# The first feed-forward layer's down products with tokens standing, and its partial sums turned back on chip

## The chip, the cores and the metric

The kernel runs on one core of one Trainium2 chip. The metric is device time in microseconds (us) of one execution. The kernel before ran three times: 843.07, 843.22 and 842.23 us, median 843.07. One further execution was recorded by the hardware profiler; its trace is the source of every other number.

In what follows PE is TensorE's matrix multiplication and PEld its weight loads, DVE is VectorE, ACT is ScalarE, POOL is GpSimd and SP is SyncE, which here only issues DMA transfers. A matmul multiplies a *standing* operand of 128 x 128, which is loaded first, with a *moving* one of up to 512 columns. The result is added up in PSUM, which has eight banks of 128 x 512 floats. SBUF is the on-chip memory that all engines read and write; HBM is the memory outside.

## The reference

One layer of a decoder trunk on 512 tokens of 1024 channels, in float32: a feed-forward layer, a token mixer, and another feed-forward layer, each between two RMS norms.

```python
def swiglu(x, w_gu, w_down):
    gate, up = jnp.split(x @ w_gu, 2, axis=-1)
    return (jax.nn.silu(gate) * up) @ w_down

# the layer, in short
x = x + 0.5 * rms_norm(swiglu(rms_norm(x, ffn1_pre_g), ffn1_w_gu, ffn1_w_down), ffn1_post_g)
h = rms_norm(x, mix_pre_g)
x = x + rms_norm(hybrid_mixer(h, ...), mix_post_g)
x = x + 0.5 * rms_norm(swiglu(rms_norm(x, ffn2_pre_g), ffn2_w_gu, ffn2_w_down), ffn2_post_g)
```

The hidden width is 2816, that is 22 chunks of 128. The mixer projects h to a recurrent branch (xl, its gates), to q and kv of a windowed attention, and to a gate gt. This case is about the down product of the first layer (`w_down`, 2816 x 1024) and about how its result reaches the residual sum.

## The kernel before

**Precision.** A product of two floats is three matmuls: each operand is split into a high part (an ACT copy into a format that PE multiplies at full rate) and a low part (a DVE subtraction), and high x high, high x low and low x high are added in PSUM.

**Layout.** Up to the end of the first layer, activations lie with channels in the 128 partitions and the 512 tokens along the row. One channel chunk of the residual stream `xT` is 128 x 512. A down product with *weights standing* gives that same layout; one with *tokens standing* gives 128 tokens by 512 channels.

**The hidden chunks come in groups** (`GROUPS1`: 0-3, 4-7, 8-11, 12-15, 16-21).

- Group 0 is computed plainly (`classic`). Its down product follows at once: for each of eight channel chunks c, four hidden chunks times three matmuls of 512 columns (lines 506 to 508), 96 in all. ACT copies each result to a stage tile and POOL sends it to HBM (line 1416), in `in_hbm`, one tile for two channel chunks. Between these products ACT and DVE make operands for the next groups (`n1.sums`, `n1.lows`), and after the fourth `xT` itself goes out to HBM (`lend`), so that its buffers can hold weights.
- Groups 1 to 4 (the first four chunks of the last) use a scheme with seven products where eight are usual, on both levels. `octo` computes gate and up with tokens standing (line 951), turns the result with DVE transposes (line 961) and stores it to HBM. While the octo of group g runs, the hidden chunks of group g-1 are read back and their sums and differences formed (`seven_forms_of`), and after it comes `seven_down` for group g-1. That is three times: for groups 1, 2 and 3.
- `seven_down` (line 1087) makes seven products into eight banks: A, B, Dd and E_, two banks each. With `by_channels` (line 1347) each product is 24 matmuls of 256 columns, weights standing. After the products named a12, s3, s2, s4, a22 and s1, ACT copies two banks to stages (line 1113) and POOL adds them to the HBM tiles (line 1116), accumulating in the transfer. The last of them goes to two places.
- After the last seven_down, a `quad` handles hidden chunks 20 and 21 (line 881, seven products of 24 matmuls), while chunks 16 to 19 come back from HBM and are split (lines 820 and 821).
- The last down product takes the six chunks 16 to 21, weights standing, channel chunk by channel chunk: c = 0 and 1 together, then 2, 3, 4. To each, `Residual.chunk` adds what the other groups had left in HBM: five reads at line 1380 and three at line 1389, of 256 KB each, issued by SP. Chunks 5 to 7 are left to `boundary`, which computes them in halves of 256 tokens: the sum of squares over all channels (line 709) closes, PE reduces it (line 550), and scaling, residual sum and the mixer's first four products (the xl weights) follow in an interleaved order.

**The order of work** is written out by hand: each engine executes in the order in which the program issues. Weights are an ordered list of *raws* (one load by SP at line 175 each, into one of five buffers) and *units* (a high part by ACT, a low part by DVE, some by POOL). `W.take` hands out the next unit and runs the splitting four units ahead. When the last unit of a raw has been split, the next raw is loaded, unless the list `W.owed` has an entry, which is then called in place of the load. Buffers are handed out in turn: a tile that asks for one waits until all readers of the tile that had it are done. `W.later` puts off a call by so many takes.

**Other work around the change.** `decay_factor` (lines 1274 to 1294, a dozen tiny DVE operations and two ACT functions) runs beside the octo of group 1. In the last down product, c = 0 loads the recurrent gates' weights (line 1309) and builds the attention masks (`masks`, lines 1324 to 1329, POOL and one DVE cast); at c = 3 the gates are split (`split_gates`, lines 1316 and 1317) and POOL reads `xT` back (`give_back`, line 1357, two transfers of 1 MB). The mixer starts with the kv product, then the convolution, whose result ACT and POOL split (line 1475) for the gate products (line 1456). The second layer's down products have tokens standing already (`by_tokens`, lines 1884 to 1886).

Of the kernel before, what the change touches and what calls it, by code (L numbers as in the profile page):

```python
# [122 lines left out]
def tile_layer(ctx: ExitStack, tc: tile.TileContext, out: bass.AP, **ins: bass.AP):  # L123
# [222 lines left out]
    for g, (f0, f1) in enumerate(GROUPS1):  # L346
        if g == 0:
            for f in range(2, f1, 2):
                add_gate_up(w1, f, "a")
        else:  # L350
            add_octo(w1, f0, "a")
            if g > 1:
                add_seven_down(ins["ffn1_w_down"], GROUPS1[g - 1][0], "a")
            if f1 < FC:
                continue
            add_quad(w1, f0 + 4, "a")
        for c in range(0, KD, 2):
            for add in add_cols(ins["ffn1_w_down"], c, f1 - f0, f"ad{g}", f0):
                add()
# [435 lines left out]
    def like(t, x):  # L795

        return t.rearrange("p (a b) -> p a b", a=2) if len(x.shape) == 3 else t

    class Hidden:


        def __init__(self, name, nxt):
            self.name, self.nxt, self.hs, self.g, self.u = name, nxt, {}, {}, {}

# [12 lines left out]
        def split(self, f):  # L817
            us, n = self.u.pop(f), f"{self.name}{f}"
            hh, hl = (spare.pop(), spare.pop()) if spare else (t2k(f"hh{n}", F32R), t2k(f"hl{n}", F32R))
            act.copy(hh, us)  # L820
            dve.tensor_sub(hl, us, hh.bitcast(F32))
            self.hs[f] = (hh, hl)

        def high(self, name, x):

            hh = t2k(f"hh{name}", F32R)
            act.copy(like(hh, x), x)
            self.forms[name] = hh, x

        def low(self, name):  # L830
# [3 lines left out]
            dve.tensor_sub(like(hl, x), x, like(hh.bitcast(F32), x))  # L834
# [171 lines left out]
        def seven_forms_of(self, f, h_hbm, at=(1, 2.5, 3.5, 4.5, 5.5, 6)):  # L1006
# [3 lines left out]
            def fetch():  # L1010
# [6 lines left out]
                z = wide(f"hx{self.name}{f}")  # L1017
                for s in range(2):
# [69 lines left out]
    def seven_down(hid, f, one, part, forms, ahead, beside={}, keep=False):  # L1088
# [7 lines left out]
        for n, (banks, form, blocks) in enumerate(((A, "a11", []), (Dd, "s3", [(1, 1)]), (B, "a12", [(0, 0)]), (A, "s2", [(1, 0)]),  # L1096
# [10 lines left out]
            for i in range(2 if form in (("s3", "s2") if keep else ("a12", "s3", "s2", "s4", "a22", "s1")) else 0):  # L1107
# [6 lines left out]
                for half, dh in blocks:  # L1114
                    o = part(half, dh, i)
                    pool.dma_start(o, st.rearrange("p (a b) -> p a b", a=2) if len(o.shape) == 3 else st, accum_op=ALU.add)  # L1116
# [217 lines left out]
    in_hbm = [hbm.tile([P, 2, 2, T // 2], F32, name=f"yp_a{i}") for i in range(KD // 2)]  # L1334

    def in_halves(t):
        return t.rearrange("p (a b) -> p a b", a=2)

    def by_channels(banks, w, h, first):

        (hi, lo), (hh, hl_) = w, h
        for m in range(4):
            o, ms = banks[m // 2][:, HALF[m % 2]], slice(m * P, (m + 1) * P)
            for k in range(2):
                js = HALF[k]
                for i, (a, x) in enumerate(((hi, hh), (hi, hl_), (lo, hh))):
                    pe.matmul(o, a[:, k, ms], x[:, js], start=first and i + k + m % 2 == 0, stop=k == 1 and i == 2, skip_group_check=True)  # L1347
# [14 lines left out]
    for g, (f0, f1) in enumerate(GROUPS1):  # L1362
        if g:
            h_hbm[f0] = hid.octo(f0, hid.seven_forms_of(before, h_hbm[before]) if g > 1 else {2: [lambda: decay.append(decay_factor())]})
            if g > 1:
                seven_down(hid, before, by_channels, lambda half, dh, i: in_hbm[2 * dh + i][:, half], hid.forms, AHEAD - 1)
            if f1 == FC:
                W.owed = [lambda: None] * 2
# [3 lines left out]
            xs = hid.last_chunks(f0, h_hbm[f0], {})  # L1372
            ka, nka = decay[0]
        else:
            xs = hid.classic(f1, banks, {})
        if f1 == FC:
            res = Residual("r1", lambda c: half_g[:, c:c + 1])
            for c in range(5):
                parts[c] = t2k(f"yp_a{c}")
                sync.dma_start(in_halves(parts[c]), in_hbm[c // 2][:, :, c % 2])  # L1380
        for c in range(KD):
            if f1 == FC and c == 0:
                load_gates()
            if f1 == FC and c == 0:
                neg = masks()
            if f1 == FC and c == 1:
                for i in range(5, KD):
                    parts[i] = t2k(f"yp_a{i}")
                    sync.dma_start(in_halves(parts[i]), in_hbm[i // 2][:, :, i % 2])
            if f1 == FC and c == 1:  # L1390
                preload(AF.Sqrt)
            if f1 == FC and c == 3:
                split_gates()
            if f1 == FC and c == 3:
                x_tiles[:] = give_back()
            if f1 == FC and c >= KD - LATE:
# [11 lines left out]
            if g == 0 and c in (0, 1, 3, 4):  # L1408
                (n1.sums if c in (0, 3) else n1.lows)(2 + c // 3)
            if g == 0 and c == 3:  # L1410
                lend(x_tiles)
                W.load(2)
            if g == 0:
                st = t2k("stage")
                act.activation(st, b, AF.Copy, scale=-1.0 if c >= KD // 2 else 1.0)
                pool.dma_start(in_hbm[c // 2][:, :, c % 2], in_halves(st))
            else:
                res.chunk(c, b, parts[c])
# [61 lines left out]
    mx.spread()  # L1480
    R = mx.R
# [563 lines left out]
```

## Time and profile before

| What | Value |
| --- | --- |
| Median of three runs | 843.07 us (842.23 to 843.22) |
| Profiled execution, own time | 842.55 us |
| Its span in the trace | 840.8 us |
| Mean granted clock of PE | 0.999 |
| PE busy | 832.2 us, 99% |
| DVE busy | 723.8 us, 86% |
| ACT busy | 520.9 us, 62% |
| POOL busy | 162.6 us, 19% |
| Layer 1's three downs on the chain start at | 155.01, 213.27 and 271.53 us |
| The quad, the last down product | 291.69 to 311.84 us, from 311.84 us on |

The page's span counts from the first to the last instruction; the device time is 1.75 us longer in this execution. An engine's share of busy time says how much room it has on average, not when. The *chain* is the sequence of work that ended last, followed back from the end of the program: an engine that stands in it with 96% could only have finished earlier by having less work, while an idle gap of another engine costs nothing. Rows of a timeline give start, duration, engine, line, operation and tiles; a bracket at the end is the idle time of that engine just before, with what ended it. Matmul rows overlap: their pace is the distance between starts.

### The profile page before, as it was taken

What the parts mean: (1) busy time and instruction counts of PE and PEld (TensorE: products, weight loads), DVE (VectorE), ACT (ScalarE), POOL (GpSimd) and SP (SyncE); (2) the same over time, 40 slices, a digit from 0 to 9 for tenths busy, and PEclk for the clock granted to TensorE, in tenths of its full rate; (3) what the DMA queues carried; (4) which work ended last, traced back from release to release, by engine and by line L of the source; (5) the groups of instructions that cost most, each with busy time, mean ns of one, the idle gap of its engine ahead of it and who ended that gap; (6) DMA issues with size and microseconds to landing.
All of it is one profiled execution on the core that took longest, in us unless ns stands there. A gap on an engine that the chain in (4) does not pass through costs nothing.

```text
span 840.8 us, 12378 instructions
## 1 busy us (share of the span) xinstructions
PE 832.2 (99%) x4504; PEld 718.9 (85%) x4504; DVE 723.8 (86%) x1026; ACT 520.9 (62%) x821; POOL 162.6 (19%) x178
## 2 busy tenths in 40 slices
PE   9999999999999999999999999999999999999996
PEld 8988888988988998987788899888888888888885
DVE  4978999998989965879889589799999899898996
ACT  6646756666666655556797456536758667666562
POOL 2023000140320333304531052002004114032001
PEclk9999999999999999999999999999999999999999
DMA  7249429398595799323511131169439939769842
GB/s 252 77 128 347 135 79 318 80 251 267 123 255 186 167 261 331 93 62 108 157 51 51 51 105 47 50 129 290 179 106 232 317 92 257 253 149 258 305 140 101
DMA packets 123614, 143.73 MB, mean 171 GB/s; under 512 B 23897, under 2 KB 81569, under 8 KB 123041
## 3 DMA queue, kind: packets, MB, share of 16 engines
q1 hardware_dynamic: 109232, 111.86, 42.0%
q0 software_dynamic: 14176, 30.94, 17.0%
q8 instruction: 35, 0.57, 0.3%
q14 instruction: 27, 0.21, 0.1%
q10 hardware_dynamic: 144, 0.13, 0.0%
HBM read 100.45 MB, written 40.89 MB: 168 GB/s over the span
## 4 chain that ended last, share of the span: by engine, by line
PE 96%; DVE 2%; DMA 1%; SPq 0%; issue 0%; ACT 0%; DVEq 0%; ACTq 0%
PE aa L951 10%; PE ab L951 10%; PE db L951 5%; PE da L951 5%; PE yaa L1347 3%; PE bb L951 3%; PE ba L951 3%; PE yda L1347 2%; PE ya L506 2%; PE ya L507 2%; PE ya L508 2%; PE aa L881 1%; PE a_first L1206 1%; PE yab L1884 1%; PE yab L1885 1%; PE yab L1886 1%
## 5 line engine op out<-in xcount | busy, mean ns | idle before, releaser
L1116 POOL DMA_DIRECT2D yp_a<-stage x42 | 36.8, 1064 | 182.6 <-ACT stage L1113 158.8
L1116 POOL DMA_DIRECT2D yp_b<-stage x42 | 36.4, 1084 | 144.3 <-ACT stage L1113 117.8
L506 PE MATMUL ya<-hha,whi_ad 128*128 128x512 f32 x62 | 24.1, 389 | 0.0
L507 PE MATMUL ya<-hla,whi_ad 128*128 128x512 f32 x62 | 24.1, 389 | 0.0
L508 PE MATMUL ya<-hha,wlo_ad 128*128 128x512 f32 x62 | 24.1, 389 | 0.0
L686 POOL TENSOR_TENSOR acca_r<-acca_r,sq_r 128x512 f32<-128x512 f32 x6 | 8.1, 1357 | 61.7 <-ACT sq_r L536 61.7
L1900 POOL DMA_DIRECT2D yp_b<-stage x8 | 4.3, 548 | 67.1 <-ACT stage L1899 67.1
L524 PE MATMUL an<-xh_mx,whi_xl 128*128 128x256 f32 x64 | 15.9, 289 | 0.0
L525 PE MATMUL an<-xh_mx,wlo_xl 128*128 128x256 f32 x64 | 15.5, 283 | 0.0
L2003 POOL TENSOR_TENSOR last<-yp,grow 128x512 f32<-128x512 f32 x3 | 3.9, 1290 | 57.2 <-DVE yp L1993 57.2
L2000 ACT ACTIVATE ysq<-yp 128x512 f32<-128x512 f32 (+1 forms) x8 | 4.8, 606 | 16.2 <-DVE yp L1993 16.2
L506 PE MATMUL gt<-xh_mx,whi_gt 128*128 128x512 f32 x32 | 14.3, 445 | 0.0
L508 PEld LDWEIGHTS ya<-hha,wlo_ad 128*128 128x128 f32 x62 | 11.6, 188 | 2.4
L506 PEld LDWEIGHTS ya<-hha,whi_ad 128*128 128x128 f32 x62 | 11.6, 188 | 2.4
L507 PEld LDWEIGHTS ya<-hla,whi_ad 128*128 128x128 f32 x62 | 11.6, 188 | 2.4
L536 ACT ACTIVATE sq_r<-yp_a 128x256 f32<-128x256 f32 (+1 forms) x10 | 5.0, 502 | 12.9 <-DVE yp_a L676 5.9
L506 PE MATMUL pq<-xh_mx,whi_q 128*128 128x512 f32 x32 | 12.8, 399 | 0.0
L506 PE MATMUL pub<-xh_f,whi_bu 128*128 128x512 f32 x32 | 12.6, 395 | 0.0
L508 PE MATMUL gt<-xh_mx,wlo_gt 128*128 128x512 f32 x32 | 12.6, 394 | 0.0
L506 PE MATMUL pgb<-xh_f,whi_bg 128*128 128x512 f32 x32 | 12.6, 393 | 0.0
L507 PE MATMUL gt<-xl_mx,whi_gt 128*128 128x512 f32 x32 | 12.6, 392 | 0.0
L508 PE MATMUL pgb<-xh_f,wlo_bg 128*128 128x512 f32 x32 | 12.5, 390 | 0.0
(2014 smaller groups left out, 3468.8 us busy)
## 6 DMA issues: line engine op xcount, KB each, us to landing
yp_a<-stage POOLq DMA_DIRECT2D x50, 256.0 KB, 9.1
yp_b<-stage POOLq DMA_DIRECT2D x50, 256.0 KB, 9.0
h_a<-za SPq DMA_DIRECT2D x16, 256.0 KB
hxa<-h_a SPq DMA_DIRECT2D x16, 256.0 KB
h_b<-zb SPq DMA_DIRECT2D x16, 256.0 KB
hxb<-h_b SPq DMA_DIRECT2D x16, 256.0 KB
xn<-in_x SPq DMA_DIRECT2D x8, 256.0 KB
xT_hbm<-xT POOLq DMA_DIRECT2D x2, 1024.0 KB, 9.8
```

The source lines that it names most:

```text
L506: pe.matmul(ps, hi[:, k, :], xh, start=start, stop=False)
L507: pe.matmul(ps, hi[:, k, :], xl, start=False, stop=False)
L508: pe.matmul(ps, lo[:, k, :], xh, start=False, stop=stop)
L524: pe.matmul(ps[:, sl], hi[:, k, :], xh, start=k == 0 and not goes_on, stop=False, skip_group_check=True)
L525: pe.matmul(ps[:, sl], lo[:, k, :], xh, start=False, stop=False, skip_group_check=True)
L881: pe.matmul(o, w[:, k, js], x, start=first and i + j + k == 0, stop=k == 3 and i == 2, skip_group_check=True)
L951: pe.matmul(b[tb], x[:, blk], w[:, k, :], start=first and q + k + j == 0, stop=q + k == 2 and j == 2, skip_group_check=True)
L1116: pool.dma_start(o, st.rearrange("p (a b) -> p a b", a=2) if len(o.shape) == 3 else st, accum_op=ALU.add)
L1206: pe.matmul(banks[j][:, HALF[0]], ws[j][part][:, k, :], n1.xs[k][xpart][:, HALF[0]], start=k == 0 and part == xpart, stop=stop and k == KD ...
L1347: pe.matmul(o, a[:, k, ms], x[:, js], start=first and i + k + m % 2 == 0, stop=k == 1 and i == 2, skip_group_check=True)
L1884: pe.matmul(banks[i], hh[:, js], hi[:, k, :], start=first and k == 0, stop=False, skip_group_check=True)
L1885: pe.matmul(banks[i], hh[:, js], lo[:, k, :], start=False, stop=False, skip_group_check=True)
```

## The change

All of layer 1's down products but the last one change to tokens standing, so that their results lie with tokens in the partitions, in eight HBM tiles `rows_hbm[tb, dh]` (token block tb of 128, half dh of the channels).

- **Group 0:** `first_down` takes 128-token blocks of the hidden chunks as standing operand and the weights, 512 channels, as moving one: two halves x four hidden chunks x four token blocks x three, again 96 matmuls of 512 columns. Its weights come in four units of two raws. The hidden chunks are split in the dealt order of tokens that the octo's results have (`in_blocks`). The work that stood between the products (`sums`, `lows`, `lend`) stands after (half, chunk) 0,1 to 1,0.
- **seven_down:** `by_dealt_tokens` makes each product of 12 matmuls of 512 columns. The hidden chunks are read back in two transfers instead of four, and read in dealt order with access patterns of four dimensions (`by_blocks`).
- **The last seven_down** is called with `hold`: products a22 and s1 are neither copied nor accumulated; their four banks stay in PSUM (`held`), which leaves out four copies and six accumulating transfers of 256 KB.
- **The eight reads of partial sums** (lines 1380 and 1389) are gone. For the first half of the channels, `read_rows(0)` reads four tiles of 256 KB at step 0 of the quad, into the tile named R and the three accumulators; `turn_sums(0)` at step 4 adds two held banks and transposes all four in blocks of 32 x 32, and `move_sums(0)` puts the blocks in place with 16 transfers of 64 KB from SBUF to SBUF, every second one by POOL, the others by SP. For the second half, `read_rows(1)` reads into a buffer of raws, `turn_sums(1)` (four adds, four transposes) stands ahead of the last down product, its target is another buffer of raws, and `move_sums(1)` stands at c = 1. `W.owed` has two loads, then `read_rows(1)`, then nothing, where it had two entries that do nothing.
- **Moved:** `decay_factor` from the octo of group 1 to that of group 2; `masks` and `split_gates` from c = 0 and c = 3 into the mixer, ahead of the convolution.

The core of the diff:

```diff
+            for dh in range(2):
+                r = W.raw(lambda dh=dh: load_raw([ins["ffn1_w_down"][0, :f1 * P, HALF_D[dh]]], f1, T, f"ad0{dh}"))
+                for i in range(0, f1, 2):
+                    add_unit(r, lambda raw, i=i: raw[:, i:i + 2, :], 2, T, f"ad0{i}{dh}")
+            continue
...
-            act.copy(hh, us)
-            dve.tensor_sub(hl, us, hh.bitcast(F32))
+            if self.in_blocks:
+                act.copy(in_turn(hh), dealt(us))
+                dve.tensor_sub(in_turn(hl), dealt(us), in_turn(hh.bitcast(F32)))
...
-            for i in range(2 if form in (("s3", "s2") if keep else ("a12", "s3", "s2", "s4", "a22", "s1")) else 0):
+            for i in range(2 if form in (("s3", "s2") if keep else ("a12", "s3", "s2", "s4") + (() if hold else ("a22", "s1"))) else 0):
...
-    def by_channels(banks, w, h, first):
-
-        (hi, lo), (hh, hl_) = w, h
-        for m in range(4):
-            o, ms = banks[m // 2][:, HALF[m % 2]], slice(m * P, (m + 1) * P)
+    def by_token_blocks(o, h, w, k, blk, start, stop):
+
+        (hh, hl_), (hi, lo) = h, w
+        for j, (x, a) in enumerate(((hh, hi), (hh, lo), (hl_, hi))):
+            pe.matmul(o, x[:, blk], a[:, k, :], start=start and j == 0, stop=stop and j == 2, skip_group_check=True)
+
+    def by_dealt_tokens(banks, w, h, first):
+
+        for i in range(2):
             for k in range(2):
-                js = HALF[k]
-                for i, (a, x) in enumerate(((hi, hh), (hi, hl_), (lo, hh))):
-                    pe.matmul(o, a[:, k, ms], x[:, js], start=first and i + k + m % 2 == 0, stop=k == 1 and i == 2, skip_group_check=True)
+                by_token_blocks(banks[i], h, w, k, slice((2 * i + k) * P, (2 * i + k + 1) * P), first and k == 0, k == 1)
+
+    def read_rows(dh):
+        if dh:
+            t = wpool.tile([P, NB * T], F32, tag="raw", name="rows_a1", bufs=NRAW)
+            row_sums[dh] = [t[:, tb * T:(tb + 1) * T] for tb in range(NB)]
+        else:
+            row_sums[dh] = [r_tile("rows_a00")] + [acc_tile(f"rows_a0{tb}") for tb in range(1, NB)]
+        for tb in range(NB):
+            sync.dma_start(row_sums[dh][tb], rows_hbm[tb, dh])
+
+    def turn_sums(dh):
+        z = wpool.tile([P, NB * T], F32, tag="raw", name="zy1", bufs=NRAW) if dh else wide("zy0")
+        for tb in range(NB):
+            row = row_sums[dh][tb]
+            if dh or tb > 1:
+                dve.tensor_add(row, row, held[tb // 2, dh][tb % 2])
+            dve.transpose(z.rearrange("p (j b n) -> p b j n", n=32, b=NB)[:, tb], row.rearrange("p (j n) -> p j n", n=32))
+        moves[dh] = z
+
+    def move_sums(dh):
+        to = wide(f"yp_a{dh}")
+        chunks = to.rearrange("p (c t) -> p c t", c=4)
+        turned = moves[dh].rearrange("p (c q n) -> p c q n", c=4, q=4)
+        for i in range(4):
+            for q in range(4):
+                (pool if q % 2 else sync).dma_start(chunks[32 * q:32 * (q + 1), :, i * P:(i + 1) * P], turned[32 * i:32 * (i + 1), :, q])
+        for c in range(4):
+            parts[4 * dh + c] = chunks[:, c]
+
+    def first_down(hs):
+
+        for dh in range(2):
+            ybanks = [bank(f"ya0{dh}{tb}") for tb in range(NB)]
+            for f in range(len(hs)):
+                if f % 2 == 0:
+                    w = W.take()
+                for tb in range(NB):
+                    by_token_blocks(ybanks[tb], hs[f], w, f % 2, slice(tb * P, (tb + 1) * P), f == 0, f == len(hs) - 1)
+                if (dh, f) in ((0, 1), (0, 2), (0, 3), (1, 0)):
+                    n = 4 * dh + f
+                    (n1.sums if n in (1, 3) else n1.lows)(2 if n < 3 else 3)
+                    if n == 3:
+                        lend(x_tiles)
+                        W.load(2)
+            for tb in range(NB):
+                st = t2k("stage")
+                act.activation(st, ybanks[tb], AF.Copy, scale=-1.0 if dh else 1.0)
+                pool.dma_start(rows_hbm[tb, dh], st)
...
-            h_hbm[f0] = hid.octo(f0, hid.seven_forms_of(before, h_hbm[before]) if g > 1 else {2: [lambda: decay.append(decay_factor())]})
+            beside = hid.seven_forms_of(before, h_hbm[before], dealt_halves=True) if g > 1 else {}
+            if g == 2:
+                beside[2] = [lambda: decay.append(decay_factor())]
+            h_hbm[f0] = hid.octo(f0, beside)
             if g > 1:
-                seven_down(hid, before, by_channels, lambda half, dh, i: in_hbm[2 * dh + i][:, half], hid.forms, AHEAD - 1)
+                held = seven_down(hid, before, by_dealt_tokens, lambda half, dh, i: rows_hbm[2 * half + i, dh], hid.forms, AHEAD - 1, hold=f1 == FC)
             if f1 == FC:
-                W.owed = [lambda: None] * 2
+                held[0, 1] = held[1, 1]
+                W.owed = [W.load, W.load, lambda: read_rows(1), lambda: None]
...
-            xs = hid.last_chunks(f0, h_hbm[f0], {})
+            xs = hid.last_chunks(f0, h_hbm[f0], {0: lambda: read_rows(0), 4: lambda: (turn_sums(0), move_sums(0))})
...
+        res = Residual("r1", lambda c: half_g[:, c:c + 1])
+        turn_sums(1)
         for c in range(KD):
-            if f1 == FC and c == 0:
+            if c == 0:
                 load_gates()
-            if f1 == FC and c == 0:
-                neg = masks()
-            if f1 == FC and c == 1:
-                for i in range(5, KD):
-                    parts[i] = t2k(f"yp_a{i}")
-                    sync.dma_start(in_halves(parts[i]), in_hbm[i // 2][:, :, i % 2])
-            if f1 == FC and c == 1:
+            if c == 1:
+                move_sums(1)
                 preload(AF.Sqrt)
...
     mx.spread()
+    neg = masks()
+    split_gates()
```

More of the change, by code (lines that the diff above doesn't have):

```diff
@@ L826, in high @@
             hh = t2k(f"hh{name}", F32R)
-            act.copy(like(hh, x), x)
+            act.copy(*by_blocks(hh, x))
             self.forms[name] = hh, x
@@ L1086, in last_chunks, with seven_down @@
             return [self.hs.pop(c) for c in range(f, f + 6)]
-    def seven_down(hid, f, one, part, forms, ahead, beside={}, keep=False):
+    def seven_down(hid, f, one, part, forms, ahead, beside={}, keep=False, hold=False):
         free = [r_tile] + 3 * [acc_tile]
@@ new lines, in tile_layer @@
+    moves = {}
+    def turn_sums(dh):
[15 more added lines that the diff above has]
+            parts[4 * dh + c] = chunks[:, c]
@@ L1407, in tile_layer @@
             b = pair_banks[c] if c < 2 else product(W.take(), xs, name=f"ya{g}{c}")
[L1408 to L1418, printed above, removed]
+            res.chunk(c, b, parts[c])
     mx = Next("mx", "mix_pre_g")
```

44 lines of the change are left out of this document (27 added, 17 removed).

## The prediction, made before the changed kernel ran

> **What bounds the kernel now.** I read the page's busy times first, then the shares of the chain that ended last.
>
> ```profile
> PE 832.2 (99%) x4504; PEld 718.9 (85%) x4504; DVE 723.8 (86%) x1026; ACT 520.9 (62%) x821; POOL 162.6 (19%) x178
> PE 96%; DVE 2%; DMA 1%; SPq 0%; issue 0%; ACT 0%; DVEq 0%; ACTq 0%
> ```
>
> TensorE (PE) is busy 99% of the span and carries 96% of the chain. So only two things move the time: PE's own work, and new gaps in it. Next the chain itself (start, us, what), at layer 1's first seven-product down and at one of layer 2's, which already has tokens standing:
>
> ```profile
> 155.01 2.87 PE yaa L1347 x24
> ...
> 166.53 2.88 PE yea L1347 x24
> ...
> 175.16 5.47 PE aa L951 x24
> ...
> 616.48 5.44 PE ab L951 x24
> ...
> 640.96 5.44 PE ab L951 x24
> ```
>
> Layer 1's down fills 155.01 to 175.16, 20.15 us in seven products of 24 matmuls with 256 columns. Layer 2's starts at 616.48 + 5.44 = 621.92 and ends at 640.96: 19.04 us.
>
> **The change, part by part**
>
> *Down products.* Each of three downs goes from 7 x 24 matmuls of 256 columns to 7 x 12 of 512, which is layer 2's form. I price it by layer 2: 20.15 - 19.04 = 1.11 us each, 3.33 us in all. A 256-column matmul takes 20.15/168 = 0.1199 us, a 512-column one 19.04/84 = 0.2267. Both lie some 13 ns above the same slope, so halving the count saves 13 ns for each of 252 matmuls.
>
> The Trainium skill ("TensorE: Matmul & The Clock Gate", Back-to-back issue gap, and the section on 56 against 53.3 ns) gives N/2.4 + 2.5 ns at the full clock. By it the whole saving would be an estimated 252 x 2.5 ns = 0.6 us, and the forecast 2.7 us higher. The 13 ns in this trace, where each matmul brings its own weights, disagree, and the trace decides.
>
> *Group 0's down* keeps 96 matmuls of 512 columns, only the operands' roles change:
>
> ```profile
> 56.93 0.39 PE L506 MATMUL ya<-hha,whi_ad 128*128 128x512 f32 x1
> 57.16 0.39 PE L507 MATMUL ya<-hla,whi_ad 128*128 128x512 f32 x1
> ```
>
> With weights standing the starts lie 0.23 us apart, layer 2's pace, so I take nothing on PE. Its hidden forms are written in dealt token order; the dealt subtraction of line 834 and the contiguous one of line 821 (below) cost 0.68 and 0.69 us. I take zero.
>
> *The decay factor* moves from the octo of group 1 to that of group 2. VectorE (DVE) rows (start, duration), then that stretch's busy times (PE, PEld, DVE, ACT, POOL), then the tightest weight and its first reader:
>
> ```profile
> 96.81 0.16 DVE L1274 TENSOR_SCALAR nabs<-cols 128x4 f32<-128x4 f32 x1
> ...
> 100.12 0.17 DVE L1294 TENSOR_SCALAR nka<-ka 128x4 f32<-128x4 f32 x1
> 116.90:163.00 46.10, 46.10 (x237) 39.55 (x236) 45.04 (x52) 28.90 (x40) 0.00 (x0) 1.00 0.49 166
> 161.27 1.21 DVE L322 TENSOR_TENSOR wlo_adt__1611<-raw_axd__1412,whi_adt__1610 128x1024 fp32r<-128x1024 f32 x1
> 162.40 0.68 DVE L834 TENSOR_TENSOR hls<-s4a,hhs 128x512 fp32r<-128x512 f32 x1
> 166.60 0.28 PE L1347 MATMUL yea<-hhs,wlo_adt__1611 128*128 128x256 f32 x1
> ```
>
> The chain takes 96.81 to 100.29, 3.5 us. In group 2 DVE is busy 45.04 of 46.10 us, so it queues there. The form hls is ready at 163.08 and PE needs it in the product that starts at 166.53: a lead of 3.4 us (the weight's is 4.1). PE arrives 0.64 us earlier (four of seven products at 1.11/7) and DVE 3.5 later: 3.4 - 0.64 - 3.5 = -0.7. I take a stall of +0.7, bounds 0 (DVE's idle microsecond of this stretch absorbs it) and 1.4 (its waits come on top). In group 1 nothing is gained, PE having no gap there.
>
> *The last quad.* Added: four 256 KB reads of rows on SyncE's queue (SP) at step 0, then at step 4 two adds and four transposes on DVE, 16 moves of 64 KB on SP and POOL. Removed: six accumulating transfers and four copies of the stages, and eight 256 KB reads on SP.
>
> ```profile
> 304.92 6.02 SPq L1380 DMA_DIRECT2D yp_a<-yp_a  x5
> 301.50 0.69 DVE L821 TENSOR_TENSOR hla<-hxa,hha 128x512 fp32r<-128x512 f32 x1 [3.58 <-ACT hha L820]
> 307.26 0.69 DVE L821 TENSOR_TENSOR hla<-hxa,hha 128x512 fp32r<-128x512 f32 x1 [2.28 <-ACT hha L820]
> 315.53 0.76 DVE L891 TENSOR_TENSOR hla<-g1a,hha 128x256 fp32r<-128x256 f32 x2 [0.47 <-ACT hha L888]
> 159.48 1.30 DVE L961 STREAM_TRANSPOSE za<-g1a 128x512 f32<-128x512 f32 x2
> 308.96 2.88 PE aa L881 x24
> ```
>
> An add or a transpose of this size is 0.68 us, so six take 4.1 us, in a stretch in which DVE idles 3.58 + 2.28 us. Behind them on DVE wait the low parts of the last two hidden chunks, which end at 316.29; PE starts the next products at 308.96 + 2.88 = 311.84 and reaches those chunks after 24 matmuls, at 317.28: slack 1.0. If the rows land by about 304, the pauses cover the six and the stall is 0; if they land only after the pauses, it is 4.1 - 1.0 = 3.1. The removed traffic was in the same queues, so I sit near the lower end: +0.2.
>
> *The boundary* (late chunks, then the mixer's first products) holds the largest term. The second half's four adds and four transposes (8 x 0.68 = 5.4 us) follow 316.29, which by now lies 2.4 us earlier, so they end near 319.3. Then eight moves go out on SP and eight on POOL. No row has these moves; POOL's nearest are:
>
> ```profile
> 397.55 0.56 POOL L1464 DMA_DIRECT2D r<-other  x1
> r<-other POOLq DMA_DIRECT2D x1, 128.0 KB, 2.6
> L1116 POOL DMA_DIRECT2D yp_a<-stage x42 | 36.8, 1064 | 182.6 <-ACT stage L1113 158.8
> ```
>
> Line 1464 is, like the moves, a plain copy inside on-chip memory: 0.56 us to issue, 2.6 to land. Eight give 319.3 + 4.5 + 2.6 = 326.4. An accumulating issue costs 1.06, which gives 330.4, the upper end. What hangs on this: the raw weight buffers go round, and the second pair of the mixer's xl weights takes the buffer from which the moves read. Its load, issued at 319.32 before, waits for all sixteen. Then:
>
> ```profile
> 319.32 0.55 SPq L175 DMA_DIRECT2D raw_xl__3440<-in_w_in  x1
> 325.74 0.37 SPq L175 DMA_DIRECT2D raw_kv<-in_w_in  x1
> 328.15 1.17 POOL L1357 DMA_DIRECT2D xT<-xT_hbm  x2
> DMA to landing us min/median/max: 6.3/7.3/8.3
> GB/s 31 27 55 106 154 181 304 379 437 365 362 372 372 516 365 352 433 437 451 437 437 437 437 437 437 382 410 437 410 355 207 137 179 207 345 335 350 319 285 276
> 333.57 1.03 ACT L210 CAST whi_xl<-raw_xl__3440 128x1024 fp32r<-128x1024 f32 x1
> 334.64 1.74 DVE L215 TENSOR_TENSOR wlo_xl<-raw_xl__3440,whi_xl 128x1024 fp32r<-128x1024 f32 x1 [0.50 <-ACT whi_xl L210]
> 339.84 0.43 DVE L709 TENSOR_TENSOR accb_r<-accb_r,sq_r 128x256 f32<-128x256 f32 x1 [0.53 <-ACT sq_r L536]
> 341.82 0.50 PE L550 MATMUL rms_r<-mean_d,accb_r 128*128 128x1 f32 x4
> ```
>
> The load (1 MB) now meets the two 1 MB reads of xT, which POOL issues behind its moves, at about the same time, and each of those took 6.3 to 8.3 us to land (third row's transfers; the 40 rates are of 326 to 338 us). Three megabytes at the 437 GB/s of that stretch are 7.2 us; with about 1.4 us to start, the weights land near 335. Bounds: 331 if they go ahead alone (the kv load, issued at 325.74, meets hardly any other traffic at first: some 5 us), 339.0 with the moves at 330.4. From the cast of these weights (333.57) to the last sum of squares (340.27) are 6.7 us, of which DVE's subtraction ran 0.5 longer than the usual 1.2: I use 6.4, since the work stands in this order on ACT and DVE. PE wants the sum at 341.82 - 3.33 + 0.7 + 0.2 = 339.4. Stall: 335.0 + 6.4 - 339.4 = 2.0; it is zero up to a landing at 333.0, and 6.0 at the upper end. Behind PE's waiting matmul stand all later products, so nothing gives it back.
>
> *Masks and gate forms* move into the mixer. POOL has the room, its chain afterwards is tight:
>
> ```profile
> 384.27 1.30 POOL L1475 TENSOR_TENSOR xcl<-xc,xch 128x512 fp32r<-128x512 f32 x1 [26.19 <-ACT xch L1474]
> 388.14 0.42 PE rg L1456
> ```
>
> The mask work fits into the 26.19 us. The gates' cast on ACT (0.6) and subtraction on POOL (1.3) come just ahead of the convolution; the first gate product starts at 388.14, when its operand has been ready since 385.57. I take +0.2; bounds 0 and 1, the share of that 1.9 us that could pass the first product's slack into the later ones.
>
> *Sum:* -3.3 + 0.7 + 0.2 + 2.0 + 0.2 = -0.2. The profiled execution took 842.55 us (span 840.8), so 842.35; the median of the runs shown is 0.52 above it: 842.9. The gain on PE is real in this account, and handed back at the boundary.
>
> **Rivals**
>
> *The boundary isn't delayed.* If the xl weights land by 333.0, the sum is -2.2 and the median 840.9. For it: PE's reader has 1.55 us of slack (340.27 to 341.82), and the weights' small packets may pass ahead of xT's. Against it: xT is issued before they have landed.
>
> *The moves are slow* (the other side). POOL's issues cost more than line 1464's. At 1.06 us each the stall is 6.0 and the sum +3.8: 846.9. It becomes slower by 1.7 us where the landing passes 336.9, that is where the moves land after 328.3: from 0.8 us for each issue on. For it: 42 issues at 1.06. Against: those accumulate into DRAM, and line 1464 does not.
>
> The Trainium skill speaks for it ("DMA: Bandwidth & Descriptors", Bandwidth): it advises batches of 1 MiB or more and puts a 64 KB transfer at 0.95 us. Eight in a row would be an estimated 7.6 us, the moves would land at 329.5 and the median be 846.0; no run here shows such moves yet, and the 0.56 us row disagrees as far as issuing goes.
>
> *The rows come late in the quad.* The stall there is 3.1 instead of 0.2; while PE stalls, the moves follow it, and the sum is about +2.7: 845.8.
>
> *The change doesn't do what it says.* PE's pace in the downs stays, because weight loads set it: the 3.3 us are not won, PE and the moves reach the boundary that much later together, and the sum is +3.1: 846.2. For it: its weight loads fill PEld in the profile's first row to 85% of the span. Against it: layer 2's 19.04 us.
>
> **How the numbers follow.** About 1.7 us (0.2%) is what a measurement of this kernel can tell from no change. Boundary delayed with a landing of 333 to 337: 0.37, its own range 841.4 to 844.8. Not delayed: 0.31. Slow moves: 0.20. Late rows: 0.08. Pace unchanged: 0.04. Faster is the second case, 0.31; slower the last three, 0.32; same the first, 0.37. The range runs from 840.0 (not delayed, and 0.9 of the 1.1 us of small stalls gone) to 847.0 (slow moves at their upper price).
>
> **What would show it.** Downs of 19.04 us in the chain; a gap ahead of line 550 in PE's rows, its releaser leading by DVE's 709 to the xl weights' load; POOL's issue times in the moves; a gap near 164 us at the fifth product of the first down. The prediction is wrong if PE waits at the boundary for something other than those weights, or if the xl load does not wait for the moves.

## The result

The changed kernel takes 840.81 us (median of 20 runs, 840.45 to 842.42) against 843.14 us before (20 runs). The ratio is 0.9975, with a 95% interval of 0.9968 to 0.9981: 2.3 us faster. A second set of runs gave 841.03 against 843.07, ratio 0.9974 (0.9964 to 0.9984). The time lies in the predicted range, but not at the forecast 842.9. It is where the first rival stood (840.9): the boundary isn't delayed.

The recorded execution of the changed kernel took 842.42 us, the slowest of its 20 runs; the one of before, 842.55, was below its median. So the two traces show less than the medians do, and I use a third, of the repeated run (841.54 us), beside them.

The page of the changed kernel, busy times and chain:

```profile
PE 831.4 (99%) x4252; PEld 706.0 (84%) x4252; DVE 733.2 (87%) x1036; ACT 517.5 (62%) x813; POOL 165.8 (20%) x188
PE 53%; issue 20%; DMA 10%; DVE 10%; ACT 4%; POOL 2%; SPq 1%; DVEq 0%; POOLq 0%; ACTq 0%
```

PE is as full as before. But in this execution the chain that ended last leaves PE: a second chain, of transfers and DVE work, has become about as long as PE's own. In the trace of the repeated run PE carries 94% of the chain again, so the two are nearly even. The table shows the stages. Each number is the time between the first PE matmul of a stage and that of the next, in us:

| Stage | Before | Changed | Changed, again |
| --- | --- | --- | --- |
| First down | 20.15 | 20.14 | 20.17 |
| Second down | 20.15 | 19.04 | 19.04 |
| Third down | 20.15 | 19.04 | 19.04 |
| Quad | 20.16 | 20.15 | 20.15 |
| Last down product, c = 0 to 4 | 20.43 | 20.71 | 20.73 |
| Late chunks to the reduction (line 550, now 555) | 9.71 | 9.99 | 9.71 |
| From there to the mixer's first product | 4.27 | 4.58 | 4.47 |
| To the first gate product | 41.98 | 41.97 | 41.97 |
| To the output product | 67.92 | 68.46 | 68.51 |
| Layer 2's first octo | 38.08 | 38.61 | 38.65 |

Two downs win 1.11 us each. The first one wins nothing. In the stages behind the quad 1.9 and 1.7 us are lost again in these two executions, more than half of it in stages whose code did not change. The medians differ by more than these traces do, so a typical execution has less of that loss, or one of before more than its trace shows.

The three downs of the changed kernel as stretches (length, then PE, PEld, DVE, ACT, POOL busy):

```profile
155.13:175.27 20.14, 20.00 (x85) 15.55 (x84) 20.14 (x25) 12.67 (x20) 5.68 (x7) 1.00 0.44 108
213.35:232.39 19.04, 19.04 (x85) 15.77 (x84) 19.00 (x23) 13.43 (x21) 7.04 (x8) 1.00 0.63 148
270.47:289.51 19.04, 19.04 (x85) 15.77 (x84) 17.26 (x21) 11.09 (x18) 5.36 (x7) 1.00 0.59 139
```

In the first row DVE is busy for the whole 20.14 us and PE is not. Its rows, PE first, then DVE:

```profile
166.21 0.50 PE L1361 MATMUL yea<-whi_adt__1592,hhs 128*128 128x512 f32 x1
166.69 0.49 PE L1361 MATMUL yea<-wlo_adt__1593,hhs 128*128 128x512 f32 x1
167.29 0.50 PE L1361 MATMUL yea<-whi_adt__1592,hls 128*128 128x512 f32 x1
133.46 0.16 DVE L1297 TENSOR_SCALAR nabs<-cols 128x4 f32<-128x4 f32 x1
...
136.76 0.17 DVE L1317 TENSOR_SCALAR nka<-ka 128x4 f32<-128x4 f32 x1
...
165.43 1.21 DVE L322 TENSOR_TENSOR wlo_adt__1593<-raw_axd__1369,whi_adt__1592 128x1024 fp32r<-128x1024 f32 x1
166.56 0.68 DVE L851 TENSOR_TENSOR hls<-s4a,hhs 128x512 fp32r<-128x512 f32 x1
```

The starts should lie 0.23 us apart. At the fifth product PE starts at 166.21, 166.69 and 167.29, each time as soon as ACT or DVE has delivered the operand: the weight's low part ends at 166.64, the form hls at 167.24. The decay chain lies 30 us earlier, at 133.46 to 136.93; since then DVE paused twice for 0.7 us, which did not pay for it.

The chain of waits of the changed kernel around the boundary (start, us, what):

```profile
282.75 12.11 DMA yr_a<-stage
294.98 9.34 DMA rows_a<-yr_a
304.34 1.28 DVE zy L1389 x2
...
321.36 2.05 DMA yp_a<-zy
...
326.82 1.45 DVE wlo_ad L215
328.29 5.76 DMA raw_xl__3189<-in_w_in
334.14 1.06 ACT whi_xl L210
...
339.88 0.44 DVE accb_r L714
340.36 0.61 PE rms_r L555 x4
```

Up to the moves, and again from the load on, this is the predicted chain: accumulating transfer, read of the rows, turning, then load of the xl weights, sums of squares, PE. The link between moves and load is not as predicted. The load does not wait for the sixteen moves: in the trace, SP's waits for them stand behind this load, ahead of the next one (kv, issued at 329.52). What releases the load is DVE's low part of the last down weights (`wlo_ad`, which ends at 328.27), and SP's own eight issues of moves had ended at 326.77. A run described below (decay factor in group 1 and xT late together) shows it without DVE's part, in SP's rows:

```profile
318.39 5.31 SPq L1398 DMA_DIRECT2D yp_a<-zy  x8
323.75 0.95 SPq L175 DMA_DIRECT2D raw_xl__3185<-in_w_in  x1
```

There the load is issued right behind SP's last move, while POOL's last move lands only at 326.34. So the moves hold the load back by the time that SP spends on issuing them, and not by their landing. ACT's first row behind the moves (323.41) also follows a DVE addition that ended at 323.37, so the landing of a move need not stand in this chain at all.

The chain's length was not as predicted either: it reaches PE at 340.32. PE's last matmul ahead starts at 339.96, so it would have been there at 340.08. The wait is 0.28 us in this trace; in the repeated one PE finds the sum ready and waits nothing.

### The profile page after: what moved, and what is told of

It reads as the page before. It is cut to its first block, busy times and chain, and to the rows that moved or that the text cites. A ratio compares the mean times of both kernels' runs of the same rounds, so it can differ in the third digit from the quotient of the medians.

```text
span 840.5 us, 11905 instructions
## 1 busy us (share of the span) xinstructions
PE 831.4 (99%) x4252; PEld 706.0 (84%) x4252; DVE 733.2 (87%) x1036; ACT 517.5 (62%) x813; POOL 165.8 (20%) x188
## 4 chain that ended last, share of the span: by engine, by line
PE 53%; issue 20%; DMA 10%; DVE 10%; ACT 4%; POOL 2%; SPq 1%; DVEq 0%; POOLq 0%; ACTq 0%
PE ab L968 10%; DMA yr_a<-stage 7%; PE db L968 5%; PE bb L968 3%; PE yab L1946 1%; PE yab L1948 1%; PE yab L1947 1%; POOL yr_a L1139 1%; DVE xc L1508 1%; DMA rows_a<-yr_a 1%; PE mn L529 1%; DMA raw_second<-in_ffn_w_gu 1%; PE an L529 1%; PE mn L530 1%; PE an L530 1%
## 5 line engine op out<-in xcount | busy, mean ns | idle before, releaser
L1139 POOL DMA_DIRECT2D yr_a<-stage x36 | 31.6, 1015 | 177.9 <-ACT stage L1136 156.8
L1398 POOL DMA_DIRECT2D yp_a<-zy x16 | 8.8, 555 | 25.8 <-DMA rows_a<-yr_a 17.5
L512 PE MATMUL pq<-xl_mx,whi_q 128*128 128x512 f32 x32 | 12.5, 391 | 0.0
L513 PE MATMUL pq<-xh_mx,wlo_q 128*128 128x512 f32 x32 | 12.5, 390 | 0.0
L513 PE MATMUL pub<-xh_f,wlo_bu 128*128 128x512 f32 x32 | 12.5, 389 | 0.0
L512 PE MATMUL pgb<-xl_f,whi_bg 128*128 128x512 f32 x32 | 12.5, 389 | 0.0
L512 PE MATMUL pub<-xl_f,whi_bu 128*128 128x512 f32 x32 | 12.5, 389 | 0.0
L1361 PE MATMUL ya<-whi_ad,hha 128*128 128x512 f32 x32 | 12.4, 389 | 0.0
```

Source lines behind the costliest of these rows:

```text
L512: pe.matmul(ps, hi[:, k, :], xl, start=False, stop=False)
L513: pe.matmul(ps, lo[:, k, :], xh, start=False, stop=stop)
L1139: pool.dma_start(o, st, accum_op=ALU.add)
L1361: pe.matmul(o, x[:, blk], a[:, k, :], start=start and j == 0, stop=stop and j == 2, skip_group_check=True)
L1398: (pool if q % 2 else sync).dma_start(chunks[32 * q:32 * (q + 1), :, i * P:(i + 1) * P], turned[32 * i:32 * (i + 1), :, q])
```

## The experiments

The runs come from three chips, on which the kernel before took 843.07, 843.04 and 842.83 us. Where a run is compared with the changed kernel, that is the repeated run (841.03 us).

**The changed kernel again.**

> The changed kernel once more, for a second trace and as the base of the others. In the recorded trace the first down takes 20.14 us and the other two 19.04, and PE waits 0.3 us for the sum of squares at the boundary. If these are the kernel's own, the new trace has the same three downs, a boundary wait below 1 us, and the median is 840.8. If the recorded layer-2 gap of 0.4 us near 594 us belonged to that one execution, it is not there again.

Measured: 841.03 us (9 runs, 839.9 to 841.68). The downs are the same to 0.03 us. The wait for the sum of squares is gone, the slow first octo of layer 2 is there again: it does not belong to one execution.

**The decay factor back in group 1.**

```diff
-            if g == 2:
+            if g == 1:
                 beside[2] = [lambda: decay.append(decay_factor())]
```

> Only the decay factor goes back beside the octo of group 1. Theory A (DVE's queue in group 2 is full, the decay chain's 3.5 us make PE wait 1.1 us in the first down): first down 19.04 us, median 1.1 below the changed kernel, 839.7. Theory B (the wait comes from the faster pace alone, DVE being busy 97% there): the first down keeps at least 0.5 us of it, median 840.3 or more. Theory C (what is won there is lost again at the boundary, where the moves set the end): first down 19.04, median 840.8.

Measured: 839.62 us (5 runs, 839.28 to 839.81), ratio to before 0.9957 (0.9945 to 0.997), so 1.4 us below the changed kernel. The first down in its trace:

```profile
154.50:173.54 19.04, 19.04 (x85) 15.77 (x84) 19.00 (x23) 13.31 (x21) 7.05 (x8) 1.00 0.63 147
```

Theory A holds: the faster pace alone leaves no wait, and the boundary doesn't take the gain back. The page's chain is PE's, with 97%. The boundary does not take the gain back because its chain comes earlier too: the xl load is issued at 326.30 instead of 327.79, and PE reaches line 555 at 338.11 instead of 339.59.

**The decay factor in group 3.** The same line with `g == 3`.

> The decay factor beside the octo of group 3 instead of group 2. There DVE was busy 32.3 of 38.1 us before the change, so by theory A (a full queue is what makes PE wait) its 3.5 us fit into pauses: first down 19.04 us, no wait in the second either, median as with group 1, 839.6. Theory B (the chain costs its time wherever seven forms are made, since these are needed in the down that follows): the wait moves to the second down, 20.1 us there, median 841.0.

Measured: 839.42 us (4 runs, 839.38 to 839.87), ratio 0.9958 (0.9944 to 0.9972); all three downs take 19.04 us. Theory A again. This and the run before are the fastest kernels of the study, and not told apart.

**The slow pace in the new layout.**

```diff
-                by_token_blocks(banks[i], h, w, k, slice(...), first and k == 0, k == 1)
+                for n, cs in enumerate(HALF):
+                    for j, (x, a) in enumerate(((hh, hi), (hh, lo), (hl_, hi))):
+                        pe.matmul(banks[i][:, cs], x[:, blk], a[:, k, cs], ...)
```

> The three downs keep tokens standing and all else of the change, but each product is made of 24 matmuls of 256 columns again. Theory A (the pace of 512 columns is the whole gain): downs of 20.15 us, the first up to 20.6 as the decay chain still crowds DVE; median 2.2 to 2.7 above the changed kernel, 843.0 to 843.5. Theory B (the gain comes from the copies and transfers left out, not from the pace): median within 1 us of the changed kernel, 841.8 or less.

Measured: 844.01 us (10 runs), ratio to before 1.001 (1.0001 to 1.0019). First and second down:

```profile
155.07:175.72 20.65, 20.43 (x170) 20.23 (x168) 20.65 (x25) 13.15 (x21) 6.23 (x8) 1.00 0.46 108
213.82:233.98 20.16, 20.16 (x170) 20.15 (x168) 19.75 (x23) 14.53 (x22) 7.02 (x8) 1.00 0.65 156
```

It is 3.0 us above the changed kernel, half a microsecond more than theory A gave at most; 2.7 of them are the downs (20.65 + 20.16 + 20.15 against 20.17 + 19.04 + 19.04). So the pace is the gain, and all else in the change together costs about 1 us. Half a microsecond of that is the decay chain even at the slow pace.

**Moves of 32 KB.**

```diff
-                (pool if q % 2 else sync).dma_start(chunks[32 * q:32 * (q + 1), :, i * P:(i + 1) * P], turned[32 * i:32 * (i + 1), :, q])
+                for cs in (HALF_C if dh else [slice(0, 4)]):
+                    (pool if q % 2 else sync).dma_start(chunks[32 * q:32 * (q + 1), cs, i * P:(i + 1) * P], turned[32 * i:32 * (i + 1), cs, q])
```

> The second half's 16 moves of 64 KB become 32 of 32 KB, the same bytes; nothing else. At 0.54 us for each issue on POOL and 0.7 on SP the moves land some 4.5 us later, near 332.7, the xl weights near 338.5. Theory A (PE's wait at the boundary hangs on that load, landing plus 6.2 us against PE at 340.1): wait 4 to 5 us, median 844.5 to 846. Theory B (the wait hangs on something else, the moves are hidden): wait as before, median 840.8.

Measured: 851.46 us (4 runs), ratio 1.0101 (1.0087 to 1.0115), twice the expected loss. Its rows of SP, POOL, ACT and PE:

```profile
320.00 12.19 SPq L1400 DMA_DIRECT2D yp_a<-zy  x16
332.30 0.53 SPq L175 DMA_DIRECT2D raw_xl__3205<-in_w_in  x1
331.31 1.14 POOL L1432 DMA_DIRECT2D xT<-xT_hbm  x2
342.44 1.04 ACT L210 CAST whi_xl<-raw_xl__3205 128x1024 fp32r<-128x1024 f32 x1 [7.86 <-DMA raw_xl__3205<-in_w_in]
348.74 0.58 PE L555 MATMUL rms_r<-mean_d,accb_r 128*128 128x1 f32 x2 [9.51 <-DVE accb_r L714]
```

The sixteen issues on SP take 12.19 us, 0.76 each, and the load stands behind them in SP's queue: it is issued 4 us later than in the changed kernel. That much was expected, though for another reason (the landing of the moves). From the cast to PE's matmul are 348.74 - 342.44 = 6.3 us, as foretold. But the load itself takes 10.0 us instead of 5.8. POOL was done first this time, so xT's reads were issued 1 us ahead of the load rather than behind it.

**xT read later, and earlier.** Two runs move `give_back` to c = 4 and to c = 2 instead of c = 3.

> The two reads of xT are issued one channel chunk later (c = 4), about 2 us after the load of the xl weights instead of 1.1 us. In the run with 32 small moves xT was issued 1 us ahead of that load and it took 9.7 us, in the changed kernel 5.5. Theory A (packets of the two queues take turns, so what is issued first decides): the load takes some 4 us, the xl weights land 1 us earlier, PE's wait at the boundary is zero; the median gains 0 to 0.3 us, 840.7 to 841.0, as PE arrived only just too early. Theory B: xT then lands too late for the residual sums, and PE waits 1 us or more in the products after the late chunks; median 842 or more.

> The changed kernel with the two reads of xT issued one channel chunk earlier (c = 2), so that POOL issues them between the moves' end and the load of the xl weights instead of 1.1 us behind that load. Theory A (what is issued first goes through: the load took 5.9 us with xT 1.1 us behind it, 5.5 with xT 4.5 us behind it, 9.7 with xT 1 us ahead of it): the load takes 9 to 10 us, the weights land near 337, PE waits 3 to 4 us for the sum of squares, median 843.5 to 845. Theory B (the 9.7 us came from the 32 small moves, not from the order): the load takes 5.5 to 6.5 us, median 840.7 to 841.3.

With xT late the median is 840.99 (7 runs, ratio to before 0.9978, 0.9968 to 0.9989). The load does not become shorter than 5.5 us, so that part of theory A missed; PE has no wait at the boundary, and as it hardly had one before, nothing is gained. With xT early the median is 847.56 us (4 runs, ratio 1.0048, 1.0032 to 1.0065). The issues of the reads (POOL) and of the load (SP), and the cast that waits for the load (ACT), in the three kernels: early first, then the changed one, then late:

```profile
327.41 1.14 POOL L1430 DMA_DIRECT2D xT<-xT_hbm  x2
328.30 0.39 SPq L175 DMA_DIRECT2D raw_xl__3189<-in_w_in  x1
338.19 1.05 ACT L210 CAST whi_xl<-raw_xl__3189 128x1024 fp32r<-128x1024 f32 x1 [5.96 <-DMA raw_xl__3189<-in_w_in]
```

```profile
329.36 1.15 POOL L1430 DMA_DIRECT2D xT<-xT_hbm  x2
328.29 0.39 SPq L175 DMA_DIRECT2D raw_xl__3189<-in_w_in  x1
334.14 1.05 ACT L210 CAST whi_xl<-raw_xl__3189 128x1024 fp32r<-128x1024 f32 x1 [2.21 <-DMA raw_xl__3189<-in_w_in]
```

```profile
326.93 0.61 SPq L175 DMA_DIRECT2D raw_xl__3185<-in_w_in  x1
331.45 1.15 POOL L1430 DMA_DIRECT2D xT<-xT_hbm  x2
332.44 1.05 ACT L210 CAST whi_xl<-raw_xl__3185 128x1024 fp32r<-128x1024 f32 x1 [0.48 <-DMA raw_xl__3185<-in_w_in]
```

The load is issued at 328.30 and 328.29 in the first two, and the cast can start 9.9 or 5.9 us later (9.8 and 5.8 by the chain of waits): what differs is whether xT is issued 0.9 us before it or 1.1 us behind it. Being 4.5 us behind (third fence, 326.93 to 332.44) makes it hardly faster. So theory A on the order is right, and theory B, that the small moves made the load slow, falls. In the late run one more thing changes: the load no longer waits for DVE's low part and is issued 1.4 us earlier. The loss of 6.5 us is larger than expected: PE waits 4.3 us for the sum, and 1.9 more up to the mixer's first product (6.41 against 4.47 us). What makes the 1.9 was not followed further.

Why the order matters so much, the transfers' packets show. First 330 to 334 us of the early run, then 330 to 333 us and 335 to 338 us of the changed kernel; software_dynamic is POOL's queue and carries xT, hardware_dynamic is SP's:

```profile
q0 software_dynamic: 209, 1.58, 94.7%
q1 hardware_dynamic: 76, 0.08, 5.5%
```

```profile
q1 hardware_dynamic: 1006, 1.01, 103.1%
q0 software_dynamic: 1, 0.01, 0.6%
```

```profile
q0 software_dynamic: 149, 1.10, 86.5%
q1 hardware_dynamic: 160, 0.16, 15.3%
```

A row gives packets, megabytes and share of time. POOL's packets hold some 7.5 KB, SP's about 1 KB. Where both queues send through the whole stretch (335 to 338 us) the packets are nearly equal in number, so SP's queue gets about an eighth of the bytes. In the early run xT's packets take nearly everything while the load waits. In the changed kernel they have hardly begun by 333 us, 3.6 us after xT's first issue, and by then the load has moved most of its megabyte.

**Group 1 and xT late together.**

> Decay factor beside group 1, and xT read one chunk later. Theory A: the first down takes 19.04 us, the boundary is not delayed by the xl weights, and the 0.7 us that PE lost between the sum of squares and the mixer's first product with the decay factor alone shrink; median 839.0 to 839.6. Theory B (xT late): 840 or more.

Measured: 839.75 us (5 runs), ratio 0.9961 (0.9947 to 0.9974): 0.15 above theory A's bound, not better than with the decay factor alone. The 0.7 us that the expectation wanted back are not there to win: the stage from the sum of squares to the mixer's first product takes 4.38 us with the decay factor alone and 4.26 here, against 4.27 before the change. In this trace layer 2's first octo took 39.01 us.

**Without the hold.**

```diff
-                held = seven_down(..., AHEAD - 1, hold=f1 == FC)
+                held = seven_down(..., AHEAD - 1)
...
-            if dh or tb > 1:
-                dve.tensor_add(row, row, held[tb // 2, dh][tb % 2])
```

> The last two results of the last seven-product down are no longer held in PSUM: four copies, six accumulating transfers of 256 KB come back, the six adds of held banks go. Theory A (holding them is needed, because the rows of the first half can only be read once the last transfer has landed, some 10 us after its issue near 290 us): rows land at 306 or later instead of 304, DVE turns them behind the time when PE wants the last two hidden chunks, a wait of 1 to 4 us in the quad or at the boundary; median 842 to 845. Theory B (the quad has room for it, and six adds less repay it): 840.6 to 841.2.

Measured: 848.48 us (5 runs), ratio 1.0073 (1.0046 to 1.0101): 7.5 us above the changed kernel, more than the 4 I gave it at most. POOL's last transfers, SP's reads and DVE's first transposes in this kernel:

```profile
296.21 4.44 POOL L1139 DMA_DIRECT2D yr_a<-stage  x5 [0.46 <-issue]
296.68 7.19 SPq L1379 DMA_DIRECT2D rows_a<-yr_a  x4
311.35 2.66 DVE L1387 STREAM_TRANSPOSE zy<-rows_a 128x512 f32<-128x512 f32 x4 [9.57 <-DMA rows_a<-yr_a]
```

The reads wait on SP for the accumulating transfers, and DVE waits 9.57 us for the rows, until 311.35 instead of 304.34. Everything behind in DVE's order, the low parts of the last hidden chunks among it, is late by as much, and PE loses 7.3 us in the first two products of the last down. Six adds fewer repay none of it.

## Why the prediction was right or wrong

- **The downs.** Right: 19.04 us in the second and third, and in the first where the decay chain is out of the way. The Trainium skill's 2.5 ns for each matmul ("TensorE: Matmul & The Clock Gate", Back-to-back issue gap) would have made it an estimated 0.6 us for all three. The run with the slow pace loses 2.7 us in the downs, with part of the first one's hidden behind the decay chain. The 13 ns for each matmul that the trace of before gave hold.
- **The decay factor.** Right in place and sign, somewhat small: +0.7 forecast (0 to 1.4), 1.1 us in the traces and 1.4 to 1.6 between the medians. DVE's idle microsecond, which was to absorb a part, absorbed nothing. Before the change DVE paused for 0.69 and 0.20 us in that stretch, in the changed kernel for 0.69 and 0.71 us, each time until an ACT copy was done. So the form hls is ready 4.2 us later than before (167.24 against 163.08), not 3.5.
- **The quad.** PE's wait of 0.2 came out as 0.3 us, in the last down product, where PE reaches the last two hidden chunks (315.13). The rows landed at 304.34, about when they had to. What I missed is on DVE: its second pause was by then nearly over, spent on waiting for these rows, and the six operations left the low parts at 315.76 instead of the 313.9 that I had reckoned with, late by 1.9 us. The slack that saved PE did not save the moves behind them, which began at 321.1, not 319.3.
- **The boundary.** This is the step that failed: a stall of 2.0 us forecast, 0.28 and 0 measured. Two links of it were wrong. First, the load was to start when all sixteen moves had landed, at 326.4. It does not wait for them, which the prediction itself names as a sign that it is wrong. SP's issues hold it to 326.8 and DVE's low part to 328.27, so it starts 1.9 us late for a reason that the prediction has not. That POOL's last move also lands then (328.10) is a coincidence. Second, the load took 5.8 us, not 8.6, because I had let xT's reads start at the same time. In the code POOL issues them behind its additions of two chunks (line 691 of the changed kernel), 1.1 us after the load, and their packets come later still. With xT ahead, the load takes 9.8 us: the size that I took belongs to the other order. The 1.4 us to start within those 8.6 stood in no row of before; in the changed kernel the load's first packet comes 1.1 us after its issue. Besides, PE came at 340.1, not 339.4: the decay chain cost 0.4 us more, and the stretch ahead of the first down was 0.3 us longer in this trace (the down starts at 155.13, before at 154.85). The errors partly cancel: the weights landed at 334.05 instead of 335.0.
- **The slow moves** did not come. Their issues in the changed kernel, SP and POOL:

```profile
321.09 5.68 SPq L1398 DMA_DIRECT2D yp_a<-zy  x8
321.36 4.33 POOL L1398 DMA_DIRECT2D yp_a<-zy  x8 [8.23 <-DVE zy L1389]
```

  POOL takes 0.54 us for each, as line 1464's 0.56 said. SP is the slower of the two, with 0.71; I had given SP no price, and it is SP's 5.68 us behind which the load stands. The Trainium skill's 0.95 us for a transfer of 64 KB ("DMA: Bandwidth & Descriptors", Bandwidth), taken one after another, would have been an estimated 7.6 us. These rows show 4.33 and 5.68 us.
- **Masks and gates.** Nothing came of the +0.2: the first gate product comes 41.97 us after the mixer's first product, before 41.98. Half a microsecond is lost further on, see below.
- **The rivals.** That the boundary isn't delayed had a chance of 0.31, against 0.37 for the forecast, and gave 840.9. The number is nearly the measured one, the reason is not, so part of the hit is luck: its landing by 333.0 was missed by 1.0 us in the recorded trace, and small packets do not pass ahead of xT's, they get the smaller share. That the change doesn't do what it says is excluded by the run at the slow pace.
- **What stays open.** The stages of the repeated trace add up to 0.6 us of gain and its recorded device time lies 1.0 us below that of before, while the medians differ by 2.0 to 2.3. Which of the small losses a typical execution has, the traces don't tell. Layer 2's first octo takes 38.08 to 39.01 us in these traces with the same code; where it is slow, PE waits for an ACT copy. What makes ACT late there I have not settled.

## What to carry to other kernels

A chain of transfers that runs beside PE has to be followed instruction by instruction along every queue it uses: here one microsecond in the order of two issues from two engines is worth 6.5 us, and it is decided by two additions that stand on POOL ahead of one of them. The wait that really holds an instruction has to be read from the trace: the load was taken to hang on the moves, and hung on SP's queue and a DVE operation. A small chain of scalar work belongs in a stage whose engine has pauses in the stretch that follows, not where it happens to be started first: moved from group 2 to group 1 or 3, the same dozen operations gave 1.4 us. And where a result is needed soon, keep its last terms on chip rather than adding them in memory: that was worth 7.5 us.

## What the runs showed of the hardware

*Two transfers that overlap don't share evenly.* The reader of the 1 MB load can start 5.4 to 5.9 us after its issue when the 2 MB from the other queue are issued 1.1 or 4.5 us behind it (six traces), and 9.9 to 10.1 us after it when they are issued about 1 us ahead (two). Where both queues send, packets of the two are about equal in number (149 and 160 in 3 us) but not in size (7.4 and 1 KB), so the one with large packets gets seven times the bytes. The second comer's packets also start late. In the changed kernel the load's first packet comes 1.1 us after its issue (329.35) and xT's 3.6 us after its own (332.96); in the early run xT's comes after 1.3 us (328.70) and the load's after 3.9 (332.24). Why it is held so long these runs do not show.

*A tiny DVE operation can wait for a whole POOL operation.* The half microsecond that the repeated run loses in the mixer starts here; this run first (DVE, POOL), then the kernel before the change:

```profile
430.67 0.63 DVE L1694 SCALAR_TENSOR_TENSOR nm<-mx,nsink 128x4 f32<-128x4 f32 x1
430.66 0.63 POOL L1721 TENSOR_SCALAR_AFFINE_SELECT pp<-pa 128x512 f32<-128x512 f32 x1 [1.86 <-DVE mx L1688]
```

```profile
432.55 0.16 DVE L1632 SCALAR_TENSOR_TENSOR nm<-mx,nsink 128x4 f32<-128x4 f32 x1
432.57 0.64 POOL L1659 TENSOR_SCALAR_AFFINE_SELECT pp<-pa 128x512 f32<-128x512 f32 x1 [1.90 <-DVE mx L1626]
```

The same operation of 128 x 4 takes 0.16 us when it starts 0.02 us ahead of POOL's, and 0.63 us, POOL's whole duration, when it starts 0.01 us behind. ACT's exponentials, which need it, start 0.73 us behind its start instead of 0.26, and PE loses 0.45 us. The Trainium skill ("SBUF — State Buffer", Terms) calls the port that DVE and GpSimd share exclusive and "held for the full instruction"; these rows agree. It is a matter of hundredths, so a change far ahead can set it off or away. In five of the eleven traces the operation starts behind POOL's, by 0.01 to 0.34 us, and ends with it; in these the stretch from the first score product to the output product takes 41.79 us, in the six others 41.32 to 41.38. The recorded trace of the changed kernel is one of the six: it loses its half microsecond earlier, ahead of the first score product, for a reason not followed here.
